# A table of priority offsets for groups of instructions, and x loaded first, in a two-block transformer kernel

## The chip, the cores and the metric

The kernel runs as one program on one core of a Trainium2 chip. The metric is the device time of one execution in microseconds (us). Three runs of the kernel before took 2918.68, 2920.89 and 2923.62 us, a median of 2920.89.

## The reference

The input x has 512 tokens of 1024 channels. The first block applies two layers of the form x + mixer(norm(x)), x + ffn(norm(x)), with a convolution mixer and a sparse attention mixer (NSA). The second block applies a state-space mixer (Mamba 2) and a stick-breaking attention mixer, each followed by a layer norm, and after each a squared-ReLU MLP with another layer norm. Cut to what matters:

```python
def reference(x, ...):
    x = first_block(x, ...)      # conv, ffn0, nsa, ffn1
    return second_block(x, ...)  # mamba, mlp0, sb, mlp1

def second_block(x, ...):
    h = x
    for layer in range(DEPTH):                     # 2
        mix = mamba2_mixer(h, ...) if layer < N_A_LAYERS else stick_breaking_attention(h, ...)
        h = layer_norm(DEEPNORM_ALPHA * h + mix, ...)
        h = layer_norm(DEEPNORM_ALPHA * h + squared_relu_mlp(h, ...), ...)
    return h

def swiglu_ffn(h, w_in, w_out):                    # ffn0, ffn1
    gate, up = jnp.split(h @ w_in, 2, axis=-1)
    return (jax.nn.silu(gate) * up) @ w_out

def conformer_conv_module(h, w_in, b_in, w_dw, b_dw, ln_g, ln_b, w_out):
    a, g = jnp.split(h @ w_in + b_in, 2, axis=-1)
    u = a * jax.nn.sigmoid(g)                      # then a causal convolution of width 31,
    ...                                            # a layer norm, silu
    return u @ w_out
```

Everything is float32.

## The kernel before, in words

x stays in SBUF for the whole program as eight tiles of 128 channels by 512 tokens (x0 to x7). The program has eight phases in the order conv, ffn0, nsa, ffn1, mamba, mlp0, sb, mlp1.

**Matrix products.** A product in float32 is made of three in the type float32r. Weights and activations are split into a high part (a copy by ScalarE, `whi`, `xh`, `hh`) and a low part (a subtraction, `wlo`, `xl`, `hl`), and `mm3` (L135 to L137) issues high x high, low x high and high x low. Each weight tile is loaded by SyncE's queue (SP) into `wraw` (`load`, L106) and split by `w`: the low part is made by VectorE or GpSimd (L96), or by an accumulating DMA that GpSimd issues (L121 to L123). Weight tiles have two buffers per pool (tags `wraw`, `whi`, `wlo`), with one or three more in some phases. PSUM has six banks for products (`mm`) and two for statistics (`st`) in the dense phases.

**The mixers.** conv multiplies the normed x by pairs of weight tiles (`pair`), gates the result, and convolves three of the eight channel tiles on VectorE and five as matmuls with tap matrices (`conv_taps`), with a layer norm at the end (`HalfNorm`). nsa makes queries and keys head by head; `stats` and `rsqrt` (L152 to L156) give the norm of a head, `spread` copies it into the tile `acc` on ScalarE (L695) and turns it by four transposes on TensorE (L698), `q_finish` scales the query (L819), `turn` swaps halves by four small DMAs, multiplies twice on GpSimd (L788, L789) and adds on VectorE (L790), and `kstack` makes the stacked query tiles `qa` and `qb` (L1542 to L1545) that the score matmuls (L1004) read. mamba and sb have their own helpers; their closing products and the layer norm after them are in `closing`.

**Who sets the order.** The program is written as one list of instructions with a priority each: a running number, lowered inside `c.pri(key)` by the offset that the dictionary `PRIO` gives for the key. At the end, class `Arrange` takes the whole list. `graph` works out what depends on what, `price` gives each instruction an estimated duration, and `schedule` plays the program through: each of the five queues (PE, ACT, DVE, POOL, SP) takes, among the instructions that are ready, the one with the lowest priority number that can start at once (for SP: the lowest that has a buffer). `room` holds an instruction back until its tiles have a buffer. The resulting order of each queue, and the order in which tiles take buffers, are then fixed by `apply` as dependencies. A changed priority thus changes the order within each engine's queue and no instruction.

**The start.** `load_x` issues the first 8 columns of the parameters, the x tiles, two halves of the first two weight tiles (`c.early`) between them, and the rest of the parameters. It stands outside any `pri`. Loads of later weights in conv stand under `conv_load`, offset 200.

Of the kernel before, what the change touches and what calls it, by code (L numbers as in the profile page):

```python
# [17 lines left out]
D = 1024  # L18
KT = 8
# [2 lines left out]
NEG = -1e30  # L22


PRIO = {"n_gates": 50, "n_kvs": 35, "n_join": -15, "n_kvf": -15, "n_kvp": -200, "n_fink": 50, "n_compo": 70,
        "n_spread": 20, "n_wout": -30, "n_cmps": 108, "n_cmpt": 10, "n_comp": 80, "n_vfin": -30, "n_finq": 10,
        "conv_stats": 300, "conv_load": 200, "conv_centre": 50, "conv_wsplit": 80, "conv_chain": -450, "conv_finish": 50, "m_convx": -30,
        "mamba_stats": 503, "m_outs": 20, "mamba_wsplit": 17, "mamba_load": 120, "m_bturn": 26, "m_decay": 515,
# [6 lines left out]
class Ctx:  # L35
    def __init__(self, tc, es, ins):
        self.tc, self.nc, self.ins = tc, tc.nc, ins
        pool = lambda name, bufs, **k: es.enter_context(tc.tile_pool(name=name, bufs=bufs, **k))
        self.const = pool("const", 1)
        self.xp = pool("xres", 1)  # L40
        self.ap = pool("acts", 1)
        self.wp = pool("wts", 2)
        self.early = []
        self.ph = ""
        self.w3, self.w4, self.wn = None, None, 0
        self.hpos = ((0, 0), (0, 7), (2, 3))
        self.sc = pool("scr", 6)
        self.sm = pool("small", 2)
        self.uid = 0
        self.edges = []  # L50
        self.weng, self.mix = None, 0
        self.sttag = "st"
        self.nk = None
        self.xs, self.head, self.dense, self.stored = None, [], None, False
        nc = self.nc
        self.ones = self.const.tile([P, P], F32, name="ones")
        nc.vector.memset(self.ones, 1.0)
        self.ident = self.const.tile([P, P], F32, name="ident")
        make_identity(nc, self.ident)
        npar = ins["par"].shape[1]  # L60
        self.par = self.const.tile([P, npar], F32, name="par")
        self.npar = npar

    def pri(self, key):

        o = PRIO.get(key)
        return self.tc.high_priority(offset=o) if o else nullcontext()
# [167 lines left out]
def load_x(c, early):  # L235

    par = lambda a, b: c.nc.sync.dma_start(c.par[:, a:b], c.ins["par"][:, a:b])
    par(0, 8)
    c.x = [c.t(c.xp, [P, S], F32, f"x{m}") for m in range(KT)]
    c.early = [c.t(c.wp, [P, 1024], F32, "wraw") for _ in early]  # L240
    for m in range(KT):
        c.nc.sync.dma_start(c.x[m], c.ins["x"][m])
        if m in (0, 3):
            sl = slice(0, 512) if m == 0 else slice(512, 1024)
            for raw, src in zip(c.early, early):
                c.nc.sync.dma_start(raw[:, sl], src[:, sl])
    par(8, c.npar)


def store_x(c):  # L250
    for m in range(KT):
        c.nc.sync.dma_start(c.ins["out"][m], c.x[m])
# [225 lines left out]
def ffn_phase(c, i, ahead=None):  # L478
    nc = c.nc
    with ExitStack() as es:  # L480
        dense_psum(c, es)
        xs = rms_split(c, f"nf{i}")

        def product(j):
            wt = c.w(c.ins[f"ffn_w_in{i}"][j])
            ps = c.t(c.pmm, [P, S], F32, "mm")
            c.proj(ps, wt, xs)
            return ps

        early = [product(0)]  # L490
        r = rms_rstd(c, lambda: early.append(product(NFF)))
        if ahead:
            ahead()
        for pc, (j0, j1) in enumerate(((0, 8), (8, 15), (15, 22))):
            hs = c.acts("hh", "hl", j1 - j0)
            for j in range(j0, j1):
                pg, pu = early or [product(j), product(NFF + j)]
                early = None
                g = c.s()
                nc.vector.tensor_tensor(g, pg, r, op=OP.mult)  # L500
                nc.scalar.activation(g, g, AF.Silu)
                u = c.s()
                nc.vector.tensor_tensor(u, pu, r, op=OP.mult)  # L503
                nc.vector.tensor_tensor(u, u, g, op=OP.mult)  # L504
                c.split(u, hs[0][j - j0], hs[1][j - j0])
            out_proj(c, f"ffn_w_out{i}", hs, 3, pc)
# [118 lines left out]
def close_dense(c):  # L625
    for e in c.dense or ():
        e.close()
    c.dense = None
# [1116 lines left out]
        closing(c, "sb_w_o", [a[4:] + b for a, b in zip(hs, late[0])], 1, "lnmix1", head)  # L1745


class Arrange:

    PE, ACT, DVE, POOL, SP, GATE = range(6)
# [4 lines left out]
    TABLES = {"Exp": ("exp", "ln"), "Tanh": ("exp", "sig", "silu", "gelu"), "Ln": ("ln",), "Silu": ("silu",), "Sin": ("silu",),  # L1757
              "Sigmoid": ("sig",), "Gelu_apprx_tanh": ("gelu",)}

    def __init__(self, tc, edges=()):  # L1760
        self.tc, self.ins = tc, [i for b in tc.nc.cur_f.blocks if b.name == tc.start_bb_name for i in b.instructions]
        n = len(self.ins)
        self.eng, self.deps, self.touch = [-1] * n, [()] * n, [()] * n
        self.tag, self.bufs, self.count, self.late = {}, {}, {}, set()
        self.graph()
        at = {i.name: j for j, i in enumerate(self.ins)}
        for a, b in edges:
            self.deps[at[b]] = tuple(set(self.deps[at[b]]) | {at[a]})
        self.cost = [self.price(j) for j in range(n)]
        self.users, self.missing = [[] for _ in range(n)], [0] * n  # L1770
        for j in range(n):
            for k in self.deps[j]:
                if self.eng[j] >= 0 and self.eng[k] >= 0:
                    self.users[k].append(j)
                    self.missing[j] += 1
# [3 lines left out]
    @staticmethod  # L1779
    def tile(a):  # L1780
        b = getattr(a, "bass_ap", None)
        return b.tensor if b is not None and type(b.tensor).__name__ == "Tile" else None

    def box(self, a):

        t, ap, width = self.tile(a), list(a.ap), 1
        for n in list(t.shape)[1:]:
            width *= n
        p0, lo = divmod(a.bass_ap.offset, width)
        p1 = p0 + (ap[0][1] - 1) * max(ap[0][0] // width, 0) + 1  # L1790
        hi = lo + sum(max(s * (n - 1), 0) for s, n in ap[1:]) + 1
        lo += sum(min(s * (n - 1), 0) for s, n in ap[1:])
        return (0, P, lo // 512 * 512, -(-hi // 512) * 512) if "PSUM" in str(t.space) else (p0, p1, lo, hi)
# [205 lines left out]

    def apply(self):  # L2000

        order, takers = self.schedule([i.bass_priority or 0 for i in self.ins])
        info = mybir.DependencyInfo(mybir.DependencyClass.NoSync, mybir.DependencyReason.SCHED_ONLY)
        for seq in order + list(takers.values()):
            for a, b in zip(seq, seq[1:]):
                if a != b:
                    self.tc.add_manual_dep(self.ins[b], self.ins[a].name, info, reason="order")
# [80 lines left out]
def build(tc, ins, phases=None):  # L2088
    ins = dict(ins)
    for n in [k for k in ins if k.rsplit("_", 1)[-1].isdigit() and k.rsplit("_", 1)[0].endswith(("out", "0", "1", "_o"))]:  # L2090
        b, p = n.rsplit("_", 1)
        ins.setdefault(b, {})[int(p)] = ins.pop(n)
    with ExitStack() as es:
        c = Ctx(tc, es, ins)
        k0 = es.enter_context(ExitStack())
        w3 = es.enter_context(ExitStack())
        phases = phases or ["conv", "ffn0", "nsa", "ffn1", "mamba", "mlp0", "sb", "mlp1"]
        kp = k0.enter_context(tc.tile_pool(name="nconst", bufs=1)) if "ffn0" in phases and "nsa" in phases else None
        load_x(c, [ins["conv_w_in"][m] for m in (0, KT)] if phases[0] == "conv" else [])
        for p, n in zip(phases, phases[1:] + [None]):  # L2100
            c.ph = p
            if p == "nsa":
                w3.close()
            elif c.w3 is None:
                c.third_w(w3)
            if p in ("conv", "nsa"):
                {"conv": conv_phase, "nsa": nsa_phase}[p](c)
                if p == "nsa":
                    k0.close()
            elif p.startswith("ffn"):  # L2110
                ffn_phase(c, int(p[-1]), (lambda: nsa_consts(c, kp)) if p == "ffn0" and kp else None)
            else:
                head = None
                if n and n.startswith("mlp"):
                    head = [ins["mlp_w1" + n[-1]][j] for j in range(5)]
                elif n == "sb":
                    head = [ins[f"sb_w_{x}"][j] for j in range(2) for x in "kq"]
                if p.startswith("mlp"):
                    mlp_phase(c, int(p[-1]), head)
                else:  # L2120
                    {"mamba": mamba_phase, "sb": sb_phase}[p](c, head)
        close_dense(c)
        if not c.stored:
            store_x(c)
    Arrange(tc, c.edges).apply()


# [14 lines left out]
```

## Time and profile before

| | us |
|---|---|
| median of the runs | 2920.89 |
| profiled execution | 2923.25 |
| its span, first to last instruction | 2921.5 |
| TensorE (PE) busy | 2789.0 |
| weight loads on TensorE (PEld) busy | 2385.0 |
| VectorE (DVE) busy | 1691.2 |
| ScalarE (ACT) busy | 1505.3 |
| GpSimd (POOL) busy | 411.6 |

The mean granted clock of TensorE over the span is 0.976 of full speed. PE busy counts time in which at least one matmul is under way, at whichever clock. By the time order of the trace the phases lie at about 0 to 250 us (conv), 250 to 600 (ffn0), 600 to 1050 (nsa), 1050 to 1350 (ffn1), 1350 to 1900 (mamba), 1900 to 2250 (mlp0), 2250 to 2550 (sb) and 2550 to the end (mlp1).

### The profile page before, as it was taken

What the parts mean: (1) busy time and instruction counts of PE and PEld (TensorE: products, weight loads), DVE (VectorE), ACT (ScalarE), POOL (GpSimd) and SP (SyncE); (2) the same over time, 40 slices, a digit from 0 to 9 for tenths busy, and PEclk for the clock granted to TensorE, in tenths of its full rate; (3) what the DMA queues carried; (4) which work ended last, traced back from release to release, by engine and by line L of the source; (5) the groups of instructions that cost most, each with busy time, mean ns of one, the idle gap of its engine ahead of it and who ended that gap; (6) DMA issues with size and microseconds to landing.
All of it is one profiled execution on the core that took longest, in us unless ns stands there. A gap on an engine that the chain in (4) does not pass through costs nothing.

```text
span 2921.5 us, 38170 instructions
## 1 busy us (share of the span) xinstructions
PE 2789.0 (95%) x14613; PEld 2385.0 (82%) x14613; DVE 1691.2 (58%) x2959; ACT 1505.3 (52%) x2344; POOL 411.6 (14%) x427
## 2 busy tenths in 40 slices
PE   8989999999899899999999999899999999899997
PEld 7878888878777788888788878788889898888887
DVE  8976444446887953444676757643335566743335
ACT  4344222336665732323886877643335788643333
POOL 0010000034223100000111122200005222200004
PEclk9989999998999999999999999899999999999998
DMA  5324323221111033232555565722335444633332
GB/s 191 121 78 131 94 91 100 90 72 53 47 47 50 26 101 98 92 100 93 134 142 133 141 159 131 191 94 97 99 94 153 118 118 96 175 102 100 94 97 92
DMA packets 98519, 309.24 MB, mean 106 GB/s; under 512 B 11680, under 2 KB 14240, under 8 KB 98336
## 3 DMA queue, kind: packets, MB, share of 16 engines
q1 hardware_dynamic: 80192, 253.71, 27.0%
q0 software_dynamic: 18144, 53.09, 9.8%
q8 instruction: 115, 1.88, 0.3%
q14 instruction: 68, 0.56, 0.1%
HBM read 246.33 MB, written 2.10 MB: 85 GB/s over the span
## 4 chain that ended last, share of the span: by engine, by line
PE 56%; ACT 4%; DMA 3%; DVE 2%; issue 2%; POOL 1%; SPq 0%; POOLq 0%; ACTq 0%; DVEq 0%
PE mm L137 17%; PE mm L135 17%; PE mm L136 17%; DMA wlo<-wraw 2%; PE z L1677 1%; PE mm L1693 1%; PE e L1441 0%; ACT whi L121 0%; DMA wraw<-ssm_w_out 0%; ACT th L95 0%; ACT wlo L122 0%; POOL wlo L123 0%; ACT s L1443 0%; DVE x L544 0%; PE mm L1048 0%
## 5 line engine op out<-in xcount | busy, mean ns | idle before, releaser
L135 PE MATMUL mm<-xh,whi 128*128 128x512 f32 (+1 forms) x2240 | 850.2, 383 | 26.1 <-ACT whi L95 12.3
L95 ACT ACTIVATE whi<-wraw 128x1024 fp32r<-128x1024 f32 (+2 forms) x358 | 365.7, 1025 | 985.6 <-PE mm L136 759.4
L137 PE MATMUL mm<-xh,wlo 128*128 128x512 f32 (+1 forms) x2240 | 852.2, 382 | 9.1 <-DMA wlo<-wraw 6.0
L136 PE MATMUL mm<-xl,whi 128*128 128x512 f32 (+1 forms) x2240 | 850.4, 381 | 2.2 <-DVE xl L549 2.2
L135 PEld LDWEIGHTS mm<-xh,whi 128*128 128x128 f32 x2240 | 425.5, 191 | 107.3 <-ACT whi L95 15.1
L137 PEld LDWEIGHTS mm<-xh,wlo 128*128 128x128 f32 x2240 | 427.1, 191 | 92.9 <-DMA wlo<-wraw 9.2
L136 PEld LDWEIGHTS mm<-xl,whi 128*128 128x128 f32 x2240 | 427.6, 191 | 79.8 <-DVE xl L549 3.1
L135 PE MATMUL mm<-hh,whi 128*128 128x512 f32 (+1 forms) x1344 | 482.6, 361 | 6.2 <-ACT whi L95 3.5
L137 PE MATMUL mm<-hh,wlo 128*128 128x512 f32 (+1 forms) x1344 | 482.9, 360 | 5.6 <-DMA wlo<-wraw 4.6
L136 PE MATMUL mm<-hl,whi 128*128 128x512 f32 (+1 forms) x1344 | 482.2, 360 | 0.9 <-DVE hl L96 0.9
L96 DVE TENSOR_TENSOR wlo<-wraw,whi 128x1024 fp32r<-128x1024 f32 (+2 forms) x277 | 327.8, 1185 | 186.5 <-ACT whi L95 183.2
L96 POOL TENSOR_TENSOR wlo<-wraw,whi 128x1024 fp32r<-128x1024 f32 (+2 forms) x81 | 186.9, 2314 | 1355.9 <-ACT whi L95 1335.0
L137 PEld LDWEIGHTS mm<-hh,wlo 128*128 128x128 f32 x1344 | 255.6, 190 | 44.0 <-DMA wlo<-wraw 5.9
L135 PEld LDWEIGHTS mm<-hh,whi 128*128 128x128 f32 x1344 | 255.3, 190 | 44.1 <-ACT hh L95 3.8
L136 PEld LDWEIGHTS mm<-hl,whi 128*128 128x128 f32 x1344 | 255.3, 190 | 37.1 <-DVE hl L96 1.4
L123 POOL DMA_DIRECT2D wlo<-wraw x126 | 109.3, 870 | 528.0 <-ACT wlo L122 402.2
L287 DVE TENSOR_TENSOR x<-x,mm 128x512 f32<-128x512 f32 x80 | 54.9, 687 | 222.2 <-PE mm L137 222.2
L121 ACT ACTIVATE whi<-wraw 128x1024 fp32r<-128x1024 f32 (+2 forms) x126 | 111.4, 885 | 91.7 <-PE mm L136 60.3
L96 DVE TENSOR_TENSOR hl<-s,hh 128x512 fp32r<-128x512 f32 (+1 forms) x120 | 87.8, 732 | 77.5 <-ACT hh L95 77.3
L122 ACT ACTIVATE wlo<-wraw 128x1024 fp32r<-128x1024 f32 (+2 forms) x126 | 110.6, 880 | 6.7 <-PE mm L136 6.3
L503 DVE TENSOR_TENSOR s<-mm,rstd 128x512 f32<-128x512 f32 x44 | 30.4, 691 | 136.0 <-PE mm L137 136.0
L95 ACT ACTIVATE hh<-s 128x512 fp32r<-128x512 f32 (+1 forms) x120 | 75.8, 632 | 41.5 <-DVE s L504 27.4
(459 smaller groups left out, 4036.4 us busy)
## 6 DMA issues: line engine op xcount, KB each, us to landing
wraw<-mlp_w SPq DMA_DIRECT2D x144, 512.0 KB
wraw<-ffn_w_in SPq DMA_DIRECT2D x88, 512.0 KB
wlo<-wraw POOLq DMA_DIRECT2D x77, 512.0 KB, 4.8
wraw<-ssm_w_in SPq DMA_DIRECT2D x48, 512.0 KB
wraw<-ffn_w_out SPq DMA_DIRECT2D x32, 448.0 KB
wlo<-wraw POOLq DMA_DIRECT2D x48, 256.0 KB, 3.8
wraw<-conv_taps SPq DMA_DIRECT2D x20, 512.0 KB
wraw<-ssm_w_out SPq DMA_DIRECT2D x40, 256.0 KB
```

Of the source, the lines that this page charges most:

```text
L95: nc.scalar.activation(hi, x, AF.Copy)
L96: (eng or nc.vector).tensor_tensor(lo, x, hi.bitcast(F32), op=OP.subtract)
L121: self.nc.scalar.activation(hi[:, :n], raw[:, :n], AF.Copy)
L122: self.nc.scalar.activation(lo[:, :n], raw[:, :n], AF.Copy, scale=-1.0)
L123: self.nc.gpsimd.dma_start(lo[:, :n], raw[:, :n], accum_op=OP.add)
L135: mm(ps, ah, bh, start=start, stop=False)
L136: mm(ps, ah, bl, start=False, stop=False)
L137: mm(ps, al, bh, start=False, stop=stop)
L287: nc.vector.tensor_tensor(c.x[m], c.x[m], ps, op=OP.add)
L503: nc.vector.tensor_tensor(u, pu, r, op=OP.mult)
L1677: nc.tensor.matmul(reg, w, part[:, ZOFF[jj]:ZOFF[jj] + S - jj * P], start=False, stop=True, skip_group_check=True)
L1693: nc.tensor.matmul(po[:, b * P:], v[:, b, :], parts[i][:, sl], start=b == 0 and i == 0, stop=b == 3 and i == 1)
```

## The change

Two things are added. First, `load_x` is called under a new key `first` with offset 3000, so that all its loads come before any other load in the SP queue. Second, a table `DUE` names, for the phases conv, nsa, mamba and sb, 161 groups of instructions and a number for each. A group is all instructions of a phase that have the same engine, the same first output tile and the same first two inputs (`group`; the tile's tag and pool without numbers, D for a tensor in HBM). The number is added to the priority of each instruction of the group before `schedule` runs: a negative one means earlier, a positive one later. `c.marks` notes where each phase begins in the list; the first mark is set after `load_x`. There are 24 groups in conv, 55 in nsa, 43 in mamba and 39 in sb, and none of them is one of POOL. Of the numbers 99 are positive, and 40 are 50 or less in size (22 of these in nsa). The cut below keeps the entries that the text speaks of.

```diff
-PRIO = {"n_gates": 50, ...
+PRIO = {"first": 3000, "n_gates": 50, ...
...
+DUE = {
+    "conv": {
+        "ACT hh1_hid y1_convy": -1770, ..., "PE mm_pmm hl1_hid whi_wts": 2170, ...
+        "SP wraw_convr D": 215, "SP x2_xres D": 5, "SP x7_xres D": -785
+    },
+    "nsa": {
+        "ACT acc_acts hr_nq": -1795, ..., "ACT qb_nq t_nq": -150, ..., "DVE hr_nq rsq_small hr_nq": -715, ...
+        "DVE qa_nq t_nq qa_nq": -300, "DVE qb_nq t_nq qb_nq": -10, ..., "DVE t_nq s_scr s_scr": -1300, ...
+        "PE mm_ps ident_const acc_acts": -765, ...
+    },
+    "mamba": {
+        "ACT wlo_wts wraw_wts": -1195, ..., "DVE rr_small rsq_small rr_small": 1970, ..., "DVE wlo_wts wraw_wts whi_wts": 445, ...
+        "PE mm_pmm hl0_hid whi_wts": 1215, ...
+    },
+    "sb": {
+        "PE mm_pmm hh2_hid whi_wts": 2125, "PE mm_pmm hh4_hid whi_wts": 2965, ...
+    },
+}
...
+        self.due = [i.bass_priority or 0 for i in self.ins]
+        for (p, lo), hi in zip(marks, [m for _, m in marks[1:]] + [n]):
+            for j in range(lo, hi):
+                self.due[j] += DUE.get(p, {}).get(self.group(j), 0)
...
+    def group(self, j):
+        name = lambda a: self.tile(a).tag.rstrip("_0123456789") if self.tile(a) is not None else "D"
+        ins, outs = [[name(a) for a in x if hasattr(a, "ap")] for x in (self.ins[j].ins, self.ins[j].outs)]
+        return " ".join([("PE", "ACT", "DVE", "POOL", "SP", "", "")[self.eng[j]], (outs or ["-"])[0]] + ins[:2])
...
-        order, takers = self.schedule([i.bass_priority or 0 for i in self.ins])
+        order, takers = self.schedule(self.due)
...
-        load_x(c, [ins["conv_w_in"][m] for m in (0, KT)] if phases[0] == "conv" else [])
+        with c.pri("first"):
+            load_x(c, [ins["conv_w_in"][m] for m in (0, KT)] if phases[0] == "conv" else [])
         for p, n in zip(phases, phases[1:] + [None]):
             c.ph = p
+            c.marks.append((p, sum(len(b.instructions) for b in tc.nc.cur_f.blocks if b.name == tc.start_bb_name)))
...
-    Arrange(tc, c.edges).apply()
+    Arrange(tc, c.edges, c.marks).apply()
```

## Rows read from the trace of the kernel before

**Rows 1.** Busy time, share of the span and instructions of each engine (page, part 1).

```profile
PE 2789.0 (95%) x14613; PEld 2385.0 (82%) x14613; DVE 1691.2 (58%) x2959; ACT 1505.3 (52%) x2344; POOL 411.6 (14%) x427
```

**Rows 2.** Windows by stage: start:end length, busy us (instructions) by engine, clock, DMA share, GB/s.

```profile
0.00:250.00 250.00, 223.47 (x1361) 199.06 (x1362) 216.51 (x383) 118.17 (x182) 23.52 (x25) 0.96 0.40 135
...
600.00:1050.00 450.00, 402.90 (x2194) 343.80 (x2195) 329.42 (x782) 262.43 (x588) 123.15 (x80) 0.93 0.17 53
1050.00:1350.00 300.00, 300.00 (x1328) 248.52 (x1328) 133.82 (x159) 85.17 (x101) 4.53 (x8) 1.00 0.30 96
1350.00:1900.00 550.00, 524.63 (x2756) 441.61 (x2755) 366.41 (x733) 403.82 (x618) 98.65 (x107) 0.98 0.59 143
...
2250.00:2550.00 300.00, 282.54 (x1766) 256.19 (x1765) 190.82 (x271) 237.25 (x303) 78.60 (x171) 0.97 0.49 122
...
2900.00:2921.50 21.50, 5.55 (x30) 4.63 (x28) 12.91 (x42) 8.46 (x22) 0.00 (x0) 0.65 0.28 98
```

**Rows 3.** Timeline, first 22 us: start, length, engine, line, operation, operands, idle before.

```profile
0.81 0.39 SPq L106 DMA_DIRECT2D wraw<-conv_w_in  x1
...
1.25 0.89 SPq L106 DMA_DIRECT2D wraw<-conv_taps  x2
...
2.66 0.44 SPq L242 DMA_DIRECT2D x<-x  x1
...
9.51 0.99 SPq L106 DMA_DIRECT2D wraw<-conv_taps  x2
...
10.30 0.80 PE L135 MATMUL mm<-xh,whi 128*128 128x512 f32 x1 [10.30 <-ACT whi L95]
```

**Rows 4.** Windows: 5 us at the start of the loads.

```profile
5.00:10.00 5.00, 0.00 (x0) 0.00 (x0) 3.82 (x4) 4.05 (x6) 0.00 (x0) 1.00 1.00 373
```

**Rows 5.** Timeline of VectorE, 21 to 42 us.

```profile
27.60 1.23 DVE L96 TENSOR_TENSOR wlo<-wraw,whi 128x1024 fp32r<-128x1024 f32 x1 [2.96 <-ACT whi L95]
...
34.20 0.69 DVE L416 TENSOR_TENSOR s<-mm,rstd 128x512 f32<-128x512 f32 x1 [2.32 <-ACT rstd L273]
```

**Rows 6.** Timeline of TensorE, layer norm of conv and the last one.

```profile
175.05 1.86 PE L336 MATMUL st<-ones,s 128*128 128x1 f32 x8 [4.51 <-DVE s L329]
...
2908.61 1.84 PE L336 MATMUL st<-ones,s 128*128 128x1 f32 x8 [4.60 <-DVE s L329]
```

**Rows 7.** Timelines of four engines around the wait at 767.70 us.

```profile
713.01 0.18 DVE L156 SCALAR_TENSOR_TENSOR hr<-rsq,hr 128x16 f32<-128x16 f32 x1
...
742.50 0.63 ACT L695 ACTIVATE acc<-hr 128x512 f32<-128x512 f32 x1
...
743.18 0.66 PE L698 MATMUL mm<-ident,acc 128*128 128x128 f32 x4 [0.31 <-ACT acc L695]
...
709.57 0.68 DVE L790 TENSOR_TENSOR hl<-s,s 64x512 f32<-64x512 f32 x1
...
754.58 0.73 DVE L819 SCALAR_TENSOR_TENSOR s<-t,qg,mm 128x512 f32<-128x512 f32 x1
...
763.34 2.82 DVE L790 TENSOR_TENSOR t<-s,s 128x512 f32<-128x512 f32 x1
...
763.09 2.52 POOL L96 TENSOR_TENSOR wlo<-wraw,whi 128x1024 fp32r<-128x1024 f32 x1
...
767.70 0.48 PE L1004 MATMUL mm<-kdh,qa 128*128 128x128 f32 x1 [8.04 <-DVE qa L1544]
```

**Rows 8.** Windows: the two longest stretches at a low clock in nsa.

```profile
710.00:730.00 20.00, 19.03 (x100) 18.84 (x101) 4.70 (x19) 8.23 (x13) 5.83 (x3) 0.62 0.16 52
760.00:780.00 20.00, 12.30 (x59) 11.34 (x59) 15.97 (x40) 8.96 (x22) 5.92 (x5) 0.66 0.17 53
```

**Rows 9.** Waits of TensorE and of the SP queue: total us, times, longest.

```profile
PE mm L137 <- DMA wlo<-wraw: 10.6, 13, 2.2
...
SPq L106 <- DMA wlo<-wraw: 592.0, 112, 15.4
```

**Rows 10.** Costliest groups (page, part 5): the issues of accumulating DMAs.

```profile
L123 POOL DMA_DIRECT2D wlo<-wraw x126 | 109.3, 870 | 528.0 <-ACT wlo L122 402.2
```

More of the change, by code (lines that the diff above doesn't have):

```diff
@@ L22 @@
 NEG = -1e30
-PRIO = {"n_gates": 50, "n_kvs": 35, "n_join": -15, "n_kvf": -15, "n_kvp": -200, "n_fink": 50, "n_compo": 70,
+PRIO = {"first": 3000, "n_gates": 50, "n_kvs": 35, "n_join": -15, "n_kvf": -15, "n_kvp": -200, "n_fink": 50, "n_compo": 70,
         "n_spread": 20, "n_wout": -30, "n_cmps": 108, "n_cmpt": 10, "n_comp": 80, "n_vfin": -30, "n_finq": 10,
@@ L49, in __init__ @@
         self.uid = 0
-        self.edges = []
+        self.edges, self.marks = [], []
         self.weng, self.mix = None, 0
@@ L1745, in sb_phase @@
         closing(c, "sb_w_o", [a[4:] + b for a, b in zip(hs, late[0])], 1, "lnmix1", head)
+DUE = {
+    "conv": {
[5 rows of a table added]
+        "PE mm_pmm ul_convu wh_convt": 200, "PE mm_pmm xh1_acts whi_wts": 560, "PE mm_pmm xh4_acts wlo_wts": 160, "SP wraw_convr D": 215,
+        "SP x2_xres D": 5, "SP x7_xres D": -785
+    },
+    "nsa": {
+        "ACT acc_acts hr_nq": -1795, "ACT hh1_hid os_nsp": 60, "ACT pr_ntp mm_ps nmx_nsp": -2940, "ACT pr_ntp pr_ntp sums_nsp": 5, "ACT pth_npp mm_ps": 5,
+        "ACT qb_nq t_nq": -150, "ACT s_scr s_scr": 130, "ACT s_scr t_nq": -235, "ACT vch_nk mm_ps": 980, "ACT whi_wts wraw_wts": 190,
+        "DVE hl0_hid os_nsp hh0_hid": -750, "DVE hl0_hid s_scr s_scr": 445, "DVE hl1_hid os_nsp hh1_hid": 400, "DVE hl1_hid s_scr s_scr": -910,
+        "DVE hr_nq rsq_small hr_nq": -715, "DVE kdl1_nkv s_scr kdh1_nkv": 445, "DVE kvl_nk hh0_hid v1_nk": -415, "DVE kvl_nk hl1_hid v1_nk": 5,
+        "DVE nmx_nsp mm_ps": -10, "DVE os_nsp mm_ps os_nsp": 10, "DVE pr_ntp pr_ntp sums_nsp": -30, "DVE qa_nq t_nq qa_nq": -300,
+        "DVE qb_nq t_nq qb_nq": -10, "DVE s_scr hh1_hid par_const": -55, "DVE s_scr hl1_hid par_const": -355, "DVE s_scr s_scr mm_ps": 35,
+        "DVE s_scr s_scr mx_nsp": 80, "DVE sums_nsp sums_nsp": -100, "DVE t_nq s_scr s_scr": -1300, "DVE tk_nk mm_ps rstd_hid": -40,
+        "DVE v1_nk mm_ps v1_nk": -20, "DVE vcl_nk mm_ps vch_nk": 65, "DVE vt0h_nconst vch_nk": -140, "DVE vt0l_nconst vcl_nk": -80,
+        "DVE x2_xres x2_xres mm_ps": -45, "DVE x4_xres x4_xres mm_ps": -10, "DVE x5_xres x5_xres mm_ps": -25, "PE mm_ps hh1_hid whi_wts": 5,
+        "PE mm_ps hl0_hid whi_wts": 10, "PE mm_ps hl1_hid whi_wts": -15, "PE mm_ps ident_const acc_acts": -765, "PE mm_ps ident_const tk_nk": 610,
[4 rows of a table added]
+    },
+    "mamba": {
+        "ACT bh_mb bf_mb": -330, "ACT cb_mb e_pe": 620, "ACT s_scr e_pe": -435, "ACT s_scr x1_xres": 480, "ACT s_scr x3_xres": 825,
+        "ACT u41_mk mm_pmm": 235, "ACT whi_wts wraw_wts": 30, "ACT wlo_wts wraw_wts": -1195, "ACT x0_xres x0_xres par_const": 195,
+        "ACT x1_xres x1_xres par_const": 220, "ACT x6_xres x6_xres par_const": 1605, "ACT xh3_acts x3_xres par_const": 640,
+        "ACT xh5_acts x5_xres par_const": 300, "DVE cy_mb u40_mk par_const": 1195, "DVE cy_mb u41_mk par_const": 370,
+        "DVE rr_small rsq_small rr_small": 1970, "DVE s_scr s_scr e_pe": 490, "DVE wlo_wts wraw_wts whi_wts": 445, "DVE x1_xres x1_xres mm_pmm": -640,
+        "DVE x4_xres st_pst x4_xres": 320, "DVE x4_xres x4_xres par_const": 630, "DVE xl6_acts x6_xres xh6_acts": -325, "DVE yt_mb yt_mb e_pe": 790,
+        "PE e_pe ch_mb prh_mb": 40, "PE e_pe ident_const rr_small": -10, "PE e_pe ident_const xf_mb": -1130, "PE e_pe mh0_mb xd1_mk": -640,
[4 rows of a table added]
+    },
+    "sb": {
+        "ACT -": 1195, "ACT hh2_hid s_scr": 475, "ACT hh5_hid s_scr": 70, "ACT qh_skv qa_skv": 60, "ACT qh_skv qb_skv": -230, "ACT s_scr mm_pmm": -1320,
+        "ACT s_scr x0_xres": 1720, "ACT th_st t_st": 85, "ACT wlo_wts wraw_wts": 15, "ACT xh3_acts x3_xres par_const": 275, "ACT xh6_acts s_scr": 1045,
+        "ACT xh7_acts x7_xres par_const": 330, "DVE acc_acts acc_acts x4_xres": 90, "DVE t_st z_pz": 850, "DVE tl_st t_st th_st": 1390,
[5 rows of a table added]
+        "PE mm_pmm xh7_acts whi_wts": 10, "PE mm_pmm xl0_acts whi_wts": 100, "PE z_pz qh_skv kb_skv": 180, "PE z_pz th_st ntri_sk": -15
+    },
+}
@@ L1758, with __init__ @@
               "Sigmoid": ("sig",), "Gelu_apprx_tanh": ("gelu",)}
-    def __init__(self, tc, edges=()):
+    def __init__(self, tc, edges=(), marks=()):
         self.tc, self.ins = tc, [i for b in tc.nc.cur_f.blocks if b.name == tc.start_bb_name for i in b.instructions]
```

18 rows, old and new, of the table DUE are left out of this document.

## The prediction

> **What bounds the kernel now.** I read the totals of the page first, then busy time by stage, then the idle time ahead of single instructions in the time order of the stages that lose time. The totals name TensorE: 2789.0 us busy of a span of 2921.5 us [rows 1]. What an order can save is therefore the 132.5 us in which TensorE had nothing, plus what it lost while its clock was granted at the lower of its two levels (1.2 instead of 2.4 GHz).
>
> The split by stage says where that is [rows 2]. The feed-forward stages are full: the row of 1050 to 1350 us has 300.00 us busy of 300.00 at clock 1.00, and the other three of this kind look like it. The table has no entry for them. The four mixer stages, which it does name, idle 26.5 (conv, 250 less 223.47), 47.1 (nsa, 450 less 402.90), 25.4 (mamba, 550 less 524.63) and 17.5 us (sb, 300 less 282.54). The last 21.5 us, after the last dense product, idle 16.0 us; they belong to a stage without entries, so they stay. A mean clock under 1.00 costs at most its shortfall times the busy time: 0.04 x 223 = 9, 0.07 x 403 = 28, 0.02 x 525 = 10.5 and 0.03 x 283 = 8.5 us.
>
> So the sum that reordering could reach is 26.5 + 9, 47 + 28, 25 + 10.5 and 17.5 + 8.5, together about 172 us, of which 10.3 us are the start. All else is matrix work that no order changes.
>
> **The start.** The weight load of the next pair and two tap loads are issued at 0.81 and 1.25, ahead of the first x at 2.66; two more tap loads, at 9.51, stand ahead of the last three x tiles [rows 3]. The first matmul waits until 10.30 for the split of the first pair's weights [rows 3]. The change puts x, the early weights and both parameter loads at offset 3000, so the three loads of 512 KB no longer go first. The queue moved 373 GB/s at that time [rows 4]: 1.57 MB / 373 GB/s = 4.2 us. Bounds: ScalarE still needs its steps behind the landing, and only the first load might count, 1.4 us; on the other side the two loads at 9.51 are also passed by the last x tiles, five loads or 7.0 us in all. I take 4.2, because TensorE, once started, is not held up by x today and runs on from 10.30.
>
> Is it given back? VectorE must then make the three splits moved behind (1.23 us each, 3.7 us) while it is needed for conv; it has waits of 2.96 and 2.32 us before it fills up, 5.3 us together [rows 5], so they are covered. If that cover is gone, 3.7 of the 4.2 us return. Late next are the weights of the second pair: behind 3.3 MB of first loads and 0.5 MB of their own they land at about 3.8 MB / 373 GB/s + 2 = 12 us; TensorE wants them after the first pair's 48 matmuls, at 0.23 us each (300 us / 1328 in the full row [rows 2]) 11 us or more after its start at about 6, so at 17. The taps come later still. The two entries of the conv table that name loads of x do nothing: the stage's mark is set after those loads.
>
> **The rest of conv.** The large wait is a chain inside the layer norm: 4.51 us at 175.05 for the sums of squares. The same step waits 4.60 us at 2908.61, at the very end, where nothing competes [rows 6]. So that is length of dependence, not order, and the table can only bring other work beside it or the last matmul before it forward. Bounds 0 to -10; I take -2, near the row that shows the same wait with no competitor.
>
> **nsa.** The largest single wait in the trace after the start is here, 8.04 us at 767.70, where TensorE wants the stacked query [rows 7]. Read the chain backwards in the same group: VectorE added the turned half at 763.34, after the start of its scaled copy at 754.58; the transposes it needs ran at 743.18, the spread that feeds these on ScalarE at 742.50, and the last step of their rsqrt ended at 713.19. So the chain stood still for 29 us in front of ScalarE's spread and 10.7 us in front of VectorE, while both did other ready work. This is order. The table has entries for just these links: the spread (ACT acc) -1795, its transposes -765, the rsqrt -715, the turn's add -1300, the stack -300 and -150. An earlier number means that a ready instruction is taken first. I take the whole stall: from 760 to 780 us, 7.7 us idle and at mean clock 0.66 at most 0.34 x 12.3 = 4.2 us more [rows 8], 12 us. What limits it: the spread has one buffer and the scratch pool six, so a spread pulled forward holds a buffer that the next head's chain wants.
>
> A port is a second limit. The add takes 2.82 us at 763.34 beside GpSimd's split at 763.09, while the same line took 0.68 us at 709.57 [rows 7]. The Trainium skill (GPSIMD Engine Reference, section 1, Specifications) says that GpSimd's SBUF interfaces are shared with VectorE, with contention for instructions that have two SBUF inputs, as the add has. The trace agrees. By this rule an earlier add only meets an earlier split, and about 2.1 us of this term would stay; by the row alone it can go. The sum goes by the row.
>
> The other large stretch, 710 to 730 us at mean clock 0.62 (0.38 x 19.0 = 7 us) [rows 8], hangs on a GpSimd chain; the table has no entry for GpSimd. Of the 63 us that are left in nsa I take a sixth, -10: 55 of the 161 entries work here, but 22 of these are shifts of 50 or less, which only break ties. Bounds for the whole stage: 0 and -45. nsa: -22.
>
> **mamba and sb.** These wait in small pieces. In mamba TensorE's largest entry in the list of waits is 13 waits, 10.6 us together, for the low part of split weights, which an accumulating DMA makes [rows 9]. Order can bring such a load forward only if a buffer is free, and the SP queue waits 592 us in total, 112 times, for the end of just these accumulations [rows 9]. I take a seventh of mamba's 36, -5, and of sb's 26, -4. Bounds 0 to -15 and 0 to -11; on the other side up to +20 (below).
>
> **The sum.** -4.2 - 2 - 22 - 5 - 4 = -37. The profiled execution took 2923.25 us (span 2921.5 and 1.75 around it); 2923.25 - 37 = 2886. The median of the runs shown is 2920.89, 2.4 us lower, so the forecast could as well be 2884; I keep 2886.
>
> **Rivals.** A, slower, by held weight buffers. Of the entries 99 are positive; large ones push back products of one half of a split: +2170 (conv), +1215 (mamba), +2125 and +2965 (sb). A product that is pushed back holds its weight buffers and bank, and the next load queues behind it on SP. Price: a wait for low weights is 10.6 / 13 = 0.8 us [rows 9]. The 46 that cancel 37 us are the point from which it decides; with 75 such waits (of 126 accumulating loads [rows 10]) it is +60 - 37 = +23, 2946. For it: the buffers are what SP waits for. Against: TensorE takes whatever is ready, and waits this way only 13 times now.
>
> B, no change beyond the start. The entries act on a plan with estimated durations; each small shift may just move a wait. Also, names that don't match would leave the table without effect. Then it is -4.2 alone, or less with the cover gone: 2919 to 2923. For it: most waits are 1 to 3 us, the size of one instruction. Against: the 8.04 us chain is ten times that.
>
> C, far more. If most waits are order, as the one at 767.70 is, half of the 162 us that do not belong to the start goes: -81 - 4 = -85, 2838.
>
> **How the numbers follow.** Forecast 2886, own range 2862 to 2910, chance 0.67; A 0.12; B 0.11; C 0.10. The range of 2850 to 2921 takes in the forecast's bounds and half of B, and leaves out A and most of C. Under 0.2%, 5.8 us, a measurement can't tell from no change. Faster: 0.67 and C, with a little of B, 0.78; same: most of B, 0.10; slower: A, 0.12.
>
> **What would show it.** The first matmul at about 6 us, and x issued ahead of any taps. TensorE's wait at the stacked query of the second group gone or under 3 us, clock about 1.00 there. Idle time of the nsa stage near 33 instead of 47 us, of mamba and sb down by a few us each. Dense stages and tail unchanged. The prediction is wrong if the waits for low weights grow past some 40, if the sum of idle time in the mixer stages stays, or if clock and idle both improve by half.

## The result and the profile after

The changed kernel takes 2889.02 us (median of 4 runs, 2886.01 to 2893.73) beside 2920.45 us (2918.68 to 2923.62) for the kernel before: ratio 0.9891, 95% interval 0.9876 to 0.9907. The forecast was 2886. The profiled execution is the longest of the four, 2893.73 us against 2923.25 before, 29.5 us less. The terms of the forecast fare worse than its sum, so the stages come first.

The page's totals after (busy time, share, instructions):

```profile
PE 2778.8 (96%) x14613; PEld 2377.1 (82%) x14613; DVE 1698.1 (59%) x2959; ACT 1500.8 (52%) x2342; POOL 416.3 (14%) x427
```

TensorE has 10.2 us less busy time for the same 14613 matmuls, and 112.9 us without work instead of 132.5 [rows 1]. So a third of the gain is pace, two thirds are idle time. The next two fences are windows from one stage's end to the next, of before and of after: conv, nsa, mamba, sb (columns as in [rows 2]); what the text says of other stages is read from the same view.

```profile
0.00:234.60 234.60, 208.59 (x1292) 186.68 (x1292) 201.66 (x350) 112.44 (x174) 22.24 (x24) 0.96 0.40 135
600.10:1021.00 420.90, 376.08 (x2083) 322.02 (x2083) 312.83 (x752) 252.93 (x576) 123.05 (x80) 0.93 0.17 49
1387.50:1886.90 499.40, 476.93 (x2518) 401.94 (x2518) 336.24 (x680) 381.07 (x580) 96.63 (x103) 0.98 0.62 146
2247.80:2540.40 292.60, 277.20 (x1746) 251.68 (x1744) 184.87 (x252) 231.94 (x292) 76.88 (x169) 0.98 0.47 118
```

```profile
0.00:225.60 225.60, 204.49 (x1292) 183.70 (x1292) 197.01 (x351) 115.91 (x177) 22.06 (x24) 0.96 0.43 141
591.10:1005.00 413.90, 375.48 (x2083) 320.46 (x2083) 315.67 (x752) 252.12 (x576) 125.61 (x80) 0.94 0.17 50
1370.90:1854.50 483.60, 468.38 (x2518) 397.06 (x2518) 343.04 (x681) 378.95 (x579) 99.13 (x103) 0.99 0.65 150
2215.10:2508.30 293.20, 278.48 (x1746) 251.72 (x1745) 187.73 (x247) 228.44 (x290) 74.43 (x167) 0.98 0.47 116
```

Read length less the first busy column. Conv is 9.0 us shorter (idle 26.0 to 21.1, the rest pace), nsa 7.0 (44.8 to 38.4), mamba 15.8 (22.5 to 15.2, and 8.5 us less busy time for the same 2518 matmuls); sb is 0.6 longer. A dense stretch (1010 to 1310 us) is full as before, 300.00 us busy of 300.00, and the last 21.7 us idle 16.1; the last dense stage is 2.2 us longer (361.6 to 363.8), as it is with the entries of sb alone (363.9).

The start, in the timeline of the SP queue and TensorE, to set against [rows 3]:

```profile
1.25 0.42 SPq L242 DMA_DIRECT2D x<-x  x1
...
5.04 2.00 SPq L242 DMA_DIRECT2D x<-x  x4
...
8.72 1.18 SPq L106 DMA_DIRECT2D wraw<-conv_taps  x2
5.79 0.80 PE L135 MATMUL mm<-xh,whi 128*128 128x512 f32 x1 [5.79 <-ACT whi L95]
```

All x loads are ahead of the taps, which go last, and the first matmul comes at 5.79 instead of 10.30 us.

The wait at the stacked query, for which the forecast took 12 us, is the last line of the next fence (timeline after: ScalarE's two spreads, the key's and the query's, the transposes behind the first, VectorE's scaled copy and additions, GpSimd's product and split, TensorE's product), against [rows 7]:

```profile
718.99 0.62 ACT L695 ACTIVATE acc<-hr 128x512 f32<-128x512 f32 x1
733.49 0.66 PE L698 MATMUL mm<-ident,acc 128*128 128x128 f32 x4
734.19 0.66 ACT L695 ACTIVATE acc<-hr 128x512 f32<-128x512 f32 x1
742.90 0.69 DVE L790 TENSOR_TENSOR tk<-s,s 128x512 f32<-128x512 f32 x1 [2.46 <-POOL s L789]
744.79 0.74 DVE L819 SCALAR_TENSOR_TENSOR s<-t,qg,mm 128x512 f32<-128x512 f32 x1
750.84 1.30 POOL L788 TENSOR_TENSOR s<-sw,sin 128x512 f32<-128x512 f32 x1 [2.46 <-DMA sw<-s]
753.40 2.81 DVE L790 TENSOR_TENSOR t<-s,s 128x512 f32<-128x512 f32 x1 [1.80 <-POOL s L789]
753.32 2.34 POOL L96 TENSOR_TENSOR wlo<-wraw,whi 128x1024 fp32r<-128x1024 f32 x1
758.01 0.69 DVE L1544 TENSOR_TENSOR qa<-t,qa 64x512 fp32r<-64x512 f32 x1
758.85 0.44 PE L1004 MATMUL mm<-kdh,qa 128*128 128x128 f32 x1 [7.10 <-DVE qa L1544]
```

The wait is there as before, 7.10 instead of 8.04 us. Its clock times look 8.85 us earlier, but the stage itself begins 9.0 us earlier: counted from the stage's start the product runs at 167.8 us after and at 167.6 before. In this pair of traces the chain was not shortened.

### The profile page after: what moved, and what is told of

Same layout as the page of the kernel before. It is cut to its first block, busy times and chain, and to the rows that moved or that the text cites. A ratio compares the mean times of both kernels' runs of the same rounds, so it can differ in the third digit from the quotient of the medians.

```text
span 2891.7 us, 38142 instructions
## 1 busy us (share of the span) xinstructions
PE 2778.8 (96%) x14613; PEld 2377.1 (82%) x14613; DVE 1698.1 (59%) x2959; ACT 1500.8 (52%) x2342; POOL 416.3 (14%) x427
```

## The experiments

Each kernel is the changed one with the lines of its diff. `DUE` is the table of offsets; with `DUE = {}` only the order of the first loads is left of the change. Times are medians, each beside runs of the kernel before on the same chip (2921.49, 2921.22 and 2920.81 us on three chips).

**x first, no table.**

```
+DUE = {}
```

> The table is empty; x and the first weights still go first. Theory (each part acts by itself): the first matmul at 5.8 us and the end of conv 4.5 us earlier than before, the total 4 to 5 us lower, 2916. Rival 1 (VectorE's tap chain sets the end of conv, so the head start is given back): first matmul at 5.8, end of conv as before, 2920. Rival 2 (the early loads alone make the 8.9 us that conv won in the changed kernel): 2911.

2919.92 us, ratio 0.9997 (0.9987 to 1.0006): no change that can be measured. The first matmul starts at 7.22 us, not at the 5.8 expected, and conv ends 5.6 us earlier; then nsa takes 425.2 instead of 420.9 us. So the gain of the start is there, and in this trace most of it is lost in nsa; one trace can't say more, since the same order gives nsa 421.8 to 432.0 us (below).

**One stage of the table at a time**, each with x first.

```
+DUE = {"nsa": DUE["nsa"]}
...
+DUE = {"mamba": DUE["mamba"]}
...
+DUE = {"sb": DUE["sb"]}
...
+DUE = {"conv": DUE["conv"]}
```

> Only the 55 entries of nsa, with x first. Theory (each part acts by itself, and the traces of the two kernels put 7.0 us on nsa): the nsa stage 7 us shorter and the start 4.5, 2909. Rival 1 (the prediction's nsa term, 22 us): 2894. Rival 2 (parts need each other, a stage's plan depends on how the stage before left the queues): nsa unchanged within 2 us, 2916.

> Only the 43 entries of mamba, with x first. Theory (each part acts by itself; the traces put 15.8 us on mamba): mamba 16 us shorter, the start 4.5, 2900. Rival 1 (the prediction's mamba term, 5 us): 2911. Rival 2 (parts need each other): mamba within 3 us of before, 2916.

> Only the 39 entries of sb, with x first. Theory (each part acts by itself; in the traces the sb stage is 0.5 us longer and the following one 2.2 us longer): 2916 to 2918, that is the start's gain alone or less. Rival (the prediction's sb term, 4 us): 2912.

> Only the 24 entries of conv, with x first. Theory (each part acts by itself; in the traces conv ends 3.7 us earlier with its table than the mean of the four kernels that have only x first): conv ends 9 us earlier than before, total 2916. Rival (parts need each other): a total that differs from this by over 5 us while the other stages keep their order, or none of the 3.7 us.

nsa: 2917.89 us, 0.9987 (0.9977 to 0.9997). mamba: 2905.68, 0.9952 (0.9937 to 0.9967). sb: 2918.21, 0.9989 (0.9974 to 1.0003). conv: 2925.67, 1.0016 (1.0002 to 1.0029). Only mamba's part is worth much by itself, 14.2 us beside x first alone. Conv's part beside x first costs 6.0 (4.4 slower than the kernel before, where x first alone is 1.6 faster). In the trace that loss is not in conv, which is 2.3 us shorter than with x first alone, but in nsa, 432.9 us, whose order differs from that of x first alone by one instruction of VectorE. The start and the four add up to less than half of the gain: 1.6 + 2.0 + 14.2 + 1.7 - 6.0 = 13.5 of 31.4 us; by the intervals each of these is known to some 3 or 4 us.

**All but nsa.**

```
+DUE.pop("nsa")
```

> The whole change without the 55 entries of nsa. Theory (each part acts by itself, nsa is worth what its entries gave alone, 2.0 us): the changed kernel's 2889 plus 2, 2891. Rival 1 (nsa is worth the 7.0 us between the two traces): 2896. Rival 2 (the prediction's 22 us): 2911.

2902.33 us, 0.9932 (0.9909 to 0.9956). So the gain without nsa's entries is 18.9 us, with them 31.4: they are worth 12.5 us in the whole change, and 2.0 beside x first alone. The 12.5 is loose: the four times are 2897.8, 2898.9, 2905.8 and 2908.2, with the median in the gap.

**conv and nsa together**, to see whether these two make the missing part.

```
+DUE = {"conv": DUE["conv"], "nsa": DUE["nsa"]}
```

> The entries of conv and nsa, with x first. conv's entries alone gave 2926 and nsa's 2918, against 2920 with x first alone. If stages add: 2924. If the nsa entries are worth as much as in the whole change (13 us between the whole change and the one without nsa): 2913. In the trace: nsa as long as with the entries of nsa alone (423 us) if stages add, 414 as in the whole change if not.

2907.05 us, 0.9942 (0.9927 to 0.9957). The pair gains 13.8 us where conv's part alone lost 4.4, so nsa's entries are worth some 18 us beside conv's. Most of the missing part is made by these two together. The six times fall into two groups, 2896.7 and 2897.0, and 2906.7 to 2908.6; the profiled execution is one of the first (nsa in 405.4 us), so its trace shows about 10 us more than the median.

**The query chain alone**, the eight entries on which the forecast's 12 us rested.

```
+DUE = {"nsa": {k: DUE["nsa"][k] for k in (
+    'ACT acc_acts hr_nq', 'ACT s_scr t_nq', 'DVE hr_nq rsq_small hr_nq',
+    'DVE t_nq s_scr s_scr', 'DVE qa_nq t_nq qa_nq', 'DVE qb_nq t_nq qb_nq',
+    'ACT qb_nq t_nq', 'PE mm_ps ident_const acc_acts')}}
```

> Of the table only eight entries of nsa: those for the links of the query's chain that the prediction counted on (spread, its transposes, rsqrt, squares, the turn's addition, the stack); x first. The prediction's nsa term: the 8 us wait at the stacked query of the second group goes, with the low clock behind it 12 us: 2908. Theory now (the scaled copy waits for a shared scratch buffer that the key's addition frees, so earlier links only wait longer in front of it): the wait stays at 6 us or more, total 2915 to 2925.

2922.94 us, 1.0001 (0.9992 to 1.0009). The wait is still there, and the key's addition still stands ahead of the query's scaled copy (timeline, VectorE and TensorE):

```profile
750.50 2.86 DVE L790 TENSOR_TENSOR tk<-s,s 128x512 f32<-128x512 f32 x1 [2.71 <-POOL s L789]
753.62 0.74 DVE L819 SCALAR_TENSOR_TENSOR s<-t,qg,mm 128x512 f32<-128x512 f32 x1
768.21 0.45 PE L1004 MATMUL mm<-kdh,qa 128*128 128x128 f32 x1 [6.49 <-DVE qa L1544]
```

**An own buffer for the scaled copy**, instead of one of the shared scratch buffers, with the table (first kernel) and without (second).

```
-            x = c.s()
+            x = c.t(k1, [P, S], F32, "xq")
...
+DUE["nsa"]["DVE t_nq xq_nk s_scr"] = DUE["nsa"]["DVE t_nq s_scr s_scr"]
```

```
-            x = c.s()
+            x = c.t(k1, [P, S], F32, "xq")
...
+DUE = {}
```

> The changed kernel, and the scaled query in nsa gets a buffer of its own in place of one of the six shared scratch buffers (its addition keeps its entry of the table). Theory (the query's chain waits for a scratch buffer, which the key's addition frees): the scaled copy runs before the key's addition, the 7.1 us wait at the stacked query of the second group falls under 3 us, total 2 to 8 us below 2889. Rival (the chain is set by the small DMAs and GpSimd behind the copy, or TensorE only runs out earlier): the wait stays at 5 us or more, the total within 3 us.

> No table; x first; the scaled query of nsa has a buffer of its own. Theory (scratch buffer): the wait at the stacked query of the second group falls from 8 us to under 4, total 4 to 10 us under the kernel with x first alone, 2910 to 2916. Rival (TensorE has too little other work there, whatever the buffer): the wait stays at 6 us or more, total 2920.

With the table: 2886.13 us, 0.9876 (0.9857 to 0.9896), 2.9 us under the changed kernel, with intervals that overlap. Without: 2916.38, 0.9989 (0.9981 to 0.9998). The timelines, first with, then without the table:

```profile
745.35 0.74 DVE L819 SCALAR_TENSOR_TENSOR xq<-t,qg,mm 128x512 f32<-128x512 f32 x1
750.37 0.68 DVE L790 TENSOR_TENSOR tk<-s,s 128x512 f32<-128x512 f32 x1
755.75 0.69 DVE L790 TENSOR_TENSOR t<-xq,s 128x512 f32<-128x512 f32 x1 [1.25 <-POOL xq L789]
758.47 0.69 DVE L1544 TENSOR_TENSOR qa<-t,qa 64x512 fp32r<-64x512 f32 x1
760.54 0.22 PE L1004 MATMUL mm<-kdh,qa 128*128 128x128 f32 x1
```

```profile
742.62 0.69 DVE L819 SCALAR_TENSOR_TENSOR xq<-t,qg,mm 128x512 f32<-128x512 f32 x1
743.76 2.85 DVE L790 TENSOR_TENSOR tk<-s,s 128x512 f32<-128x512 f32 x1
755.24 2.82 DVE L790 TENSOR_TENSOR t<-xq,s 128x512 f32<-128x512 f32 x1
759.96 0.45 PE L1004 MATMUL mm<-kdh,qa 128*128 128x128 f32 x1 [7.41 <-DVE qa L1544]
```

The buffer does turn the order round: the copy now goes ahead of the key's addition. But with the table the stacked query (L1544) is written at 758.47, 166.1 us into the stage, against 166.9 both before and after. The wait is gone because TensorE has other matmuls up to the product at 760.54 (20.00 us busy from 741 to 761), 1.4 us after the query is written, not because the query is there sooner; idle time comes back right behind (4.8 us from 760 to 780), and nsa idles 34.0 instead of 38.4 us. Without the table the query is written at 164.2, and the wait is 7.41 us. So the size of this wait tells little of what the stage would gain.

**The table's numbers shuffled within each stage.**

```
+for _n, _d in enumerate(DUE.values()):
+    _v = np.random.default_rng(_n).permutation(list(_d.values()))
+    _d.update((k, int(v)) for k, v in zip(list(_d), _v))
```

> The same 161 groups and the same numbers, but within each stage the numbers are dealt out to the groups at random; x first. Theory (the gain is in which group has which number): a loss, 15 us or more over 2920, since positive numbers on chain links make TensorE wait. Rival (any disturbance of the hand-set order does as well, or the entries hardly bind): within 6 us of 2920 or of 2889.

3198.16 us, 1.0946 (1.0923 to 1.0969). mamba takes some 200 us more. Its totals, and the largest of TensorE's waits:

```profile
PE 2902.1 (91%) x14613; PEld 2453.0 (77%) x14613; DVE 1706.8 (53%) x2959; ACT 1514.2 (47%) x2354; POOL 411.9 (13%) x427
```

```profile
PE mm L137 <- DMA wlo<-wraw: 42.6, 32, 3.8
```

The wait for low weights grows from 13 to 32 times [rows 9], but it is the smaller part: 113 us are busy time of the same matmuls (mean clock 0.939 instead of 0.976), 162 us idle time from many sources.

**Mamba's three weight-split entries alone.** They are the ScalarE copies (high part +30, low part -1195) and VectorE's low part (+445).

```
+DUE = {"mamba": {k: DUE["mamba"][k] for k in ('ACT whi_wts wraw_wts',
+    'ACT wlo_wts wraw_wts', 'DVE wlo_wts wraw_wts whi_wts')}}
```

> Of the table only mamba's three entries for splitting weights (low part copied by ScalarE 1195 earlier, high part 30 later, VectorE's low part 445 later); x first. Theory 1 (mamba's 14 us come from weights that are split in time): mamba 8 us or more shorter, total 2912 or less. Theory 2 (they come from the order of TensorE's and VectorE's own work, the state products and the norm at the end): mamba within 4 us of 497, total 2916 or more.

2911.4 us, 0.9966 (0.9954 to 0.9978): a gain of 9.4 us, 7.8 beyond x first, of the 14.2 that all of mamba's entries give. TensorE's waits in mamba, the largest of this kernel, then of the changed one:

```profile
PE mm L137 <- DMA wlo<-wraw: 7.7, 9, 1.8
```

```profile
PE mm L137 <- DMA wlo<-wraw: 11.2, 8, 2.7
```

With the three entries the waits for low weights are 7.7 us, against 13.3 in this stage with x first alone. In the changed kernel they are 11.2, so that part is spent again; instead most of TensorE's smaller waits there are gone (before: 2.9 us for L156 and four others of 1.3 to 1.8; after: one of 1.5, one of 1.1 and three of 0.2).

**The same order, another time.** The kernels with x first alone, with mamba's and with sb's entries issue the work up to the end of nsa in the same order on every queue; those with x first and with sb's entries differ nowhere before sb. Windows: 30 us of nsa, x first; the whole stage and the same 30 us, mamba and sb:

```profile
594.50:1019.70 425.20, 379.18 (x2083) 325.63 (x2083) 313.85 (x752) 252.72 (x576) 123.22 (x80) 0.92 0.17 49
709.50:739.50 30.00, 29.61 (x186) 28.43 (x186) 11.80 (x34) 16.98 (x38) 7.12 (x3) 0.81 0.17 53
```

```profile
596.10:1017.90 421.80, 374.95 (x2083) 321.58 (x2083) 314.53 (x752) 252.79 (x576) 123.00 (x80) 0.93 0.17 49
711.10:741.10 30.00, 29.61 (x185) 27.92 (x185) 14.58 (x41) 19.73 (x42) 8.29 (x4) 0.86 0.18 54
```

```profile
594.50:1026.50 432.00, 383.00 (x2083) 327.36 (x2083) 315.46 (x753) 253.13 (x576) 123.12 (x80) 0.91 0.17 48
709.70:739.70 30.00, 29.40 (x147) 28.79 (x147) 7.46 (x20) 12.28 (x23) 7.08 (x3) 0.59 0.18 53
```

The stage takes 425.2, 421.8 and 432.0 us. In the 30 us TensorE is busy 29.4 to 29.6 us in all three, but finishes 186, 185 and 147 matmuls, at clock 0.81, 0.86 and 0.59. A stage's time in one trace is thus known to some 10 us at best, and the entries of nsa and conv are to be judged by medians. The changed kernel and the one with conv's and nsa's entries also issue one order up to the end of ffn1; nsa takes 413.9 and 405.4 us there.

## Why the prediction was right, and where it was not

**The start: right in size, in part by luck.** -4.2 was forecast for the loads, 4.51 us is the shift of the first matmul. With x first alone it is 3.1 (7.22 us); the other 1.4 come with conv's entries, for which the forecast had nothing here: with them alone the first matmul runs at 5.96. They let ScalarE load its function table before x lands, not after (timelines of x first alone, then of the changed kernel):

```profile
4.12 1.28 ACT L210 ACT_TABLE_LOAD   x1 [4.12 <-DMA x<-x]
```

```profile
0.80 1.28 ACT L193 ACT_TABLE_LOAD   x1 [0.80 <-PEq L2197]
```

That the start is not given back in conv holds: conv and the dense stage behind it end 3.6 to 9 us earlier in every kernel with x first but the shuffled one. What the forecast missed is that an earlier start alone need not reach the end: with it alone the total falls by 1.6 us, which can't be told from nothing.

**The rest of conv: right about the wait, -2 a little small.** The layer norm's wait is the same to 0.01 us, as at the end (timeline after, against [rows 6]); conv as a whole gained 4.5 us beside the start, nearly all of it pace (4.1 us of busy time):

```profile
166.47 1.87 PE L336 MATMUL st<-ones,s 128*128 128x1 f32 x8 [4.51 <-DVE s L329]
...
2878.68 1.84 PE L336 MATMUL st<-ones,s 128*128 128x1 f32 x8 [4.60 <-DVE s L329]
```

**nsa: the step that failed.** "I take the whole stall", 12 us of the -22. The stall stayed: 7.10 us, and the 20 us around it still run at clock 0.66 (window after, against [rows 8]):

```profile
751.00:771.00 20.00, 12.90 (x55) 11.46 (x54) 15.75 (x45) 8.35 (x19) 4.97 (x4) 0.66 0.14 48
```

The error was to read the 29 us in front of ScalarE's spread as order, work that was ready and not taken. These are the rows of before that I should have had beside it (ScalarE and TensorE):

```profile
713.22 0.63 ACT L695 ACTIVATE acc<-hr 128x512 f32<-128x512 f32 x1 [1.19 <-DVE hr L156]
741.81 0.66 PE L698 MATMUL mm<-ident,acc 128*128 128x128 f32 x4
742.50 0.63 ACT L695 ACTIVATE acc<-hr 128x512 f32<-128x512 f32 x1
```

The spread at 742.50 begins as the transposes of the spread ahead of it end (741.81 + 0.66 = 742.47). It waited for their buffer, the one buffer that the forecast named as a limit and then did not price. After the change it is the same: transposes at 733.49, spread at 734.19. But the transposes themselves stood still, from the end of the key's spread to 741.81 before and to 733.49 after. The code of `room` says why (cut):

```python
if len(f) < len(r) or max(r) >= begun[tag] + len(r):
    return None
```

`begun` counts the tiles of a tag that have taken a buffer, and `r` holds the places in the program of the tiles that ask. So the tiles of one tag take their buffers in the order of the program, in every kernel here, and no offset changes that. The bank of the key's transposes stands right behind that of the product with the compressed keys, L1064 (timeline of TensorE, before, then after):

```profile
741.00 0.19 PE L1064 MATMUL mm<-kc,qa 128*128 128x64 f32 x1
```

```profile
733.35 0.30 PE L1064 MATMUL mm<-kc,qa 128*128 128x64 f32 x1 [0.78 <-DVE kc L96]
```

So the offsets on the spread and on its transposes could not bring them ahead of that product. The transposes run 141.7 us into the stage before and 142.4 after. The scaled copy is a second link of the kind: its scratch tile stands in the program behind the two that take the key's result, which need the key's addition. By the plan that the code makes, a scratch tile is free there and the copy is held back by its place alone; this is the rule that the expectations call a wait for a buffer which the key's addition frees. The own-buffer kernel takes the copy out of it: the order turns, and the total is 2.9 us lower, less than the intervals tell apart. A kernel without the rule was not tried, so that it is the first cause is read from the code and the traces and not shown by a run.

The place in the stage depends on the clock too. The kernel with conv's and nsa's entries issues nsa in the same order as the changed one, and its trace has the product 159.3 us into the stage, behind a wait that is shorter but there:

```profile
751.35 0.45 PE L1004 MATMUL mm<-kdh,qa 128*128 128x128 f32 x1 [4.97 <-DVE qa L1544]
```

From the scaled copy to the addition, 8.6 us in the changed kernel, the chain also has a swap of halves by DMA, for which the table has no entry; GpSimd's product (750.84) waited 2.46 us for it.

In this trace the port limit was the better of the two readings. The addition still takes 2.81 us beside GpSimd's split at 753.32, and 0.69 us at 742.90 where GpSimd stands still: the 2.1 us that the sum let go stayed. The Trainium skill (GPSIMD Engine Reference, section 1, Specifications), which has VectorE's instructions with two SBUF inputs contend with GpSimd, agrees with both. The 2.1 us need not stay: in the trace of conv's and nsa's entries the addition takes 0.69 us at 746.70, ahead of the split at 747.37.

The -10 for the rest of nsa was nearer: idle time fell by 6.4 us in the profiled pair. By medians nsa's entries are worth 12.5 us in the whole change, so the stage is over-forecast by some 9 us (they are worth 2.0 and some 18 us in other company).

**mamba: mis-sized.** -5 forecast, 15.8 measured in the trace and 14.2 for the entries alone, at the edge of the bound of -15. A seventh of what could be reached was too little for two reasons. The queue's wait for accumulations did stay, as argued (590.3 us, 113 times, against [rows 9]):

```profile
SPq L106 <- DMA wlo<-wraw: 590.3, 113, 19.9
```

but the step ahead of the accumulation, ScalarE's low copy, could be taken earlier: the three split entries together are worth 7.8 us. And 8.5 us are less busy time, where the forecast's seventh left 1.5 for the clock; of these the table's part is unsure, since the stage is busy 470.2 to 477.4 us in the traces without entries for mamba and 468.4 to 469.8 in those with all of them.

**sb: -4 forecast, nothing in the profiled pair.** With sb's entries alone, and without nsa's, the stage takes 286.9 us, 5.7 less than before, and the dense stage behind it gives 2.3 to 2.4 back; in the changed kernel sb takes 293.2. The total with sb's entries alone moves by 3.3 us with an interval that holds zero. Whether they gain in the changed kernel stays open.

**The rivals.** A's place is real in so far as shuffled offsets cost 277 us, but only 32 of these are the wait that A priced, and in this table low weights are waited for 10 times instead of 13, far from 75. B falls: the start alone is 2919.92, the change 2889.02. C falls: idle time went down by 20 us and not by half.

So the sum, -37 against -29.5 in the profiled pair, came out near because nsa's 15 us too many and mamba's 11 too few stood against each other, with smaller misses in conv (2.5 too few) and sb (4.6 too many). That is luck.

**What stays open.** Why nsa's entries are worth some 18 us beside conv's and 2.0 without. One part is that they don't give one order: the plan enters nsa in another state with conv's entries, and all five queues issue the stage in another order, with 37.9 us idle and 367.5 busy there, against 47.0 and 375.7 with nsa's entries alone. Another is the granted clock and where the stage's stretches at low clock fall, which differ even in one order: conv's entries alone, the base of the 18, have nsa in 432.9 us. What each part is worth, and what picks the stretch, no run here tells.

## What to carry to other kernels

Before a stall is put down to order, look for what ended just before the late instruction started: if it is another tile's reader (here 0.03 us before), it may be a buffer, and then read in the code who hands out buffers, and in which order; an offset on the late instruction does nothing there. Count a chain from the start of its stage, not of the program; a stall that only moves with the stage has not changed. Judge a table of offsets by medians of the whole and by leaving parts out, since the parts don't add up.

## What was not expected of the hardware

One order of instructions gives one stage 421.8 to 432.0 us, mostly through the clock granted in it (busy time 375.0 to 383.0 us, idle time 46.0 to 49.0), and one kernel two groups of times 10 us apart (2897 and 2907) on one chip. The kernel before, on the same chip, spreads over 11 us (2914.95 to 2926.21) without such groups.
